# Weight sums of a Strassen stage by accumulating transfers, and product sums kept in PSUM

## The chip, the cores and the metric

The kernel runs on one core of a Trainium2 chip. The metric is the device time of one execution, in microseconds (us). Three executions of the kernel before gave a median of 2241.27 us, between 2237.95 and 2241.97.

## The reference

One step of a two-layer decoder on 576 tokens (512 of a prompt, 64 of samples) of width 1024. What matters here, per layer:

```
P = RMSNorm(x) @ w_in                      # the last columns: 4 gate blocks of 1024
up_b = o_b @ w_branch[b]                   # b = 0..3, o_b 256 wide
x += (sum_b sigmoid(G_b) * up_b) @ w_out
g, u = split(RMSNorm(x) @ w_ffn_in)        # 2816 columns each
x += (silu(g) * u) @ w_ffn_out
```

All is float32. The kernel forms each product from float16 halves: a value is a high half and a low half, and a product is three matmuls (high by high, high by low, low by high) that accumulate in PSUM.

## The kernel before, in words

Activations lie transposed: 128 features in the partitions, the 576 tokens in two halves of 288 columns (`h0`, `h1`). `self.h[k]` holds the normed input's halves for feature block k.

Two stages of each layer use one level of Strassen's scheme (Winograd's form): the last gates (`last_gates`, 8 pairs of gate columns: four of block `rt`, q = 2, then four of block `rw`, q = 3) and most of the first FFN product (`ffn`, 19 pairs: a block of g and the block of u that belongs to it). A pair has weights a11, a12, a21, a22 (each 128 x 512 numbers, 256 KB, loaded by SP) and four results of 128 x 288. Seven products, each of 12 matmuls with 288 columns, take the place of eight. Their names in the code are those of their weights: A11, A12, A22, S1, S2, S3, S4.

- `strassen_weights` (line 1684) makes the seven weights. Each is split: ScalarE (ACT) scales it into the high half (line 1692), VectorE (DVE) takes the difference as the low half (1693). Between the splits stand four sums of weights, each in place: one by an accumulating DMA that GpSimd (POOL) issues (1698), three by `tensor_tensor` on POOL (1696). A sum may only start when the split of the tile that it overwrites has been made. It is a generator; its steps are called between the products.
- `strassen` (1708) issues the seven products. ACT copies the first out of PSUM (`sp1`, 1739); seven DVE additions (`plus`, 1734) make the four results, each reading one product in PSUM.
- In the FFN, `gated` (1757) takes Silu of a g result on ACT, multiplies by u on DVE and splits the product. In the gates, a tanh is taken in place and, when a pair's four results are done, four small products with `w_branch` (`ub`, 6 matmuls each) follow; DVE multiplies, POOL adds into `mg`.
- `strassen_tokens` and `tokens_gen` make the four sums of token blocks that are the other side of the products, by differences.

Buffers: PSUM has 8 banks, four in ring `b`, two each in `g` and `r`. The FFN's weight halves have the ring `u` (23 buffers, 8 of them `self.h`). The raw weights of an odd FFN pair fill both buffers of ring `rd` (a11 with a12, a21 with a22); those of an even pair lie in three of the four `raw` buffers and one of `w`.

Loops run over pairs. While pair i's products run, the next pair's weights are made and the raw weights of the one after are loaded. The framework lays down one order of instructions for each engine when the program is built, ahead of the run, by when it takes them to be ready and by their place in the source; each engine then works through its list in that order. During the first gate pairs of a layer, the chain of the RWKV recurrence is interleaved.

Of the kernel before, what the change touches and what calls it, by code (L numbers as in the profile page):

```python
# [174 lines left out]
class Net:  # L175
# [1287 lines left out]
    def tokens_gen(self):  # L1463
# [5 lines left out]
        for k in range(4):  # L1469
            y = []  # L1470
            for o in (0, 4):
                for h in (slice(0, HW), slice(HW, T)):
                    y.append(self.t("gt", [128, HW], "mty"))
                    nc.gpsimd.tensor_tensor(y[-1], self.h[k + o][:, 0, h], self.h[k + o][:, 1, h], op=ADD)
            b11, b12, b21, b22 = y
            for i, (dst, a, b) in enumerate(((b11, b12, b11), (b12, b22, b12), (b22, b22, b11), (b21, b21, b22))):
                nc.vector.tensor_tensor(dst, a, b, op=SUB)
                t = T4[2 * (0, 2, 1, 3)[i] + k // 2][:, k % 2]
                self.split(t[:, 0], t[:, 1], dst)
            yield  # L1480

    def last_gates(self, l):
# [15 lines left out]
        def branch(bi, m):  # L1498

            out = []  # L1500
            for k in range(2):
                raw = self.t("gt", [128, 256], "braw")
                nc.sync.dma_start(out=raw, in_=t["w_branch"][l, bi][128 * k:128 * k + 128, 128 * m:128 * m + 256])
                hl = self.t("gt", [128, 2, 256], "bhl", F16)
                nc.scalar.activation(hl[:, 0], raw, AF.Copy, scale=WS)
                nc.vector.scalar_tensor_tensor(hl[:, 1], raw, WS, hl[:, 0], op0=MUL, op1=SUB)
                out.append((hl[:, 0], hl[:, 1]))
            return out
        self.sw = {}
        prep = [self.strassen_weights(i, lambda bi=p[1], m=p[3]: load(bi, m), "gs", A12="u") for i, p in enumerate(pairs)]  # L1510
        next(prep[0])
        wb = branch(pairs[0][1], 0)
        yield
        for _ in range(4):
            next(prep[0])
        yield
        for i, (q, bi, name, m) in enumerate(pairs):
            if i + 1 < len(pairs):
                next(prep[i + 1])

            def steps():
                for s in range(7):
                    if s < 4:
                        next(prep[i])
                    if s > 2 and i + 1 < len(pairs):
                        next(prep[i + 1])
                    yield
            c = yield from self.strassen(self.sw[i], lambda j, k: [self.T4[2 * j + k // 2][:, k % 2, p] for p in range(2)],
                                         steps(), "b" if q == 2 else "r", "e", lambda a: nc.scalar.activation(a, a, AF.Tanh, scale=0.5 * PH))
            nwb = branch(pairs[i + 1][1], pairs[i + 1][3]) if i + 1 < len(pairs) else None  # L1530
            for j, half in ((0, 0), (1, 1), (1, 0), (0, 1)):
                hs = slice(half * HW, half * HW + HW)
                th, mg = c[2 * j + half], self.mg[m + j]
                if q == 3 and half == j:
                    self.mh[m + j] = self.t("rs" if m < 6 else "u", [128, 2, T], f"mh{m + j}", F16)
                ps = self.psum("b", [128, HW], "ub")
                run(self.gemm(ps, lambda k: wb[k], range(2), 128 * j, 128, self.hl_rhs(self.bo[name], half)))
                u = self.t("e", [128, HW], "gu")
                nc.vector.scalar_tensor_tensor(u, th, 1.0, ps, op0=ADD, op1=MUL)  # L1539
                nc.gpsimd.tensor_tensor(mg[:, hs], mg[:, hs], u, op=ADD)  # L1540
                if q == 3:
                    mh = self.mh[m + j]
                    self.split(mh[:, 0, hs], mh[:, 1, hs], mg[:, hs], 0.5 * PA * AS)
                yield
            wb = nwb
# [119 lines left out]

    def strassen_tokens(self):
# [5 lines left out]
        for k in range(4):  # L1672
            b11, b12, b21, b22 = (self.x[k + o][:, h] for o in (0, 4) for h in (h0, h1))
            for i, (dst, a, b) in enumerate(((b11, b12, b11), (b12, b22, b12), (b22, b22, b11), (b21, b21, b22))):
                nc.gpsimd.tensor_tensor(dst, a, b, op=SUB)
                src.append(((0, 2, 1, 3)[i], k, dst))
        yield out
        for i in (3, 1, 0, 2):
            for j, k, dst in src:
                if i == j:  # L1680
                    self.split(out[i][:, k, 0], out[i][:, k, 1], dst)
            yield out

    def strassen_weights(self, key, load, ring, **rings):
# [22 lines left out]

    def strassen(self, w, t, prep, ps3, ring, then=None):
# [5 lines left out]
        def product(ring, a, rhs):  # L1714
            ps = self.psum(ring, [128, HW], "fs" + a)
            for k in range(4):
                hi, lo = rhs(k)
                nc.tensor.matmul(ps, w[a][:, 0, k], hi, start=k == 0, stop=False)  # L1718
                nc.tensor.matmul(ps, w[a][:, 0, k], lo, start=False, stop=False)  # L1719
# [223 lines left out]
```

## Time and profile before

| | |
|---|---|
| three runs, median (lowest to highest) | 2241.27 us (2237.95 to 2241.97) |
| the profiled execution: time, span | 2235.82 us, 2234.1 us |
| its mean granted TensorE clock | 0.975 |
| busy: PE, DVE, ACT, POOL | 92%, 75%, 48%, 29% of the span |

Times in the trace count from the span's start. PE is the matmul engine; its records overlap, since matmuls are pipelined, so its pace is read from successive starts. "[0.42 <-DVE sc L1734]" behind an instruction is the idle time before it and what ended it. The gate stage of the first layer lies from 536.1 to 682.0 us, its FFN pairs from 781.5 to 987.1; in the second layer they lie from 1629.4 to 1776.5 and from 1878.2 to 2086.5.

### The profile page before, as it was taken

Reading aid. Unit: us, or ns where it says so; the run is one execution under the profiler, and the core shown is the slowest. Engines: PE = TensorE matmul, PEld = TensorE weight load, DVE = VectorE, ACT = ScalarE, POOL = GpSimd, SP = SyncE. Lnnn points to the kernel's source line nnn. Section 1 sums busy time; section 2 is a strip of 40 time slices with the busy share of each in tenths; the row PEclk is TensorE's granted clock in tenths of the full one; section 3 lists DMA queues with packets and bytes.
Section 4 is the critical chain, followed back from the end, with each engine's and each line's share of the span. In section 5 each row is a group of like instructions: output and inputs, shape, how many; then the busy total and the mean of one; then the engine's idle time right before and its main releaser. Section 6 shows DMA issues by size and latency. Waiting matters only on the chain.

```text
span 2234.1 us, 42266 instructions
## 1 busy us (share of the span) xinstructions
PE 2047.3 (92%) x15754; PEld 1616.7 (72%) x15754; DVE 1677.4 (75%) x3719; ACT 1070.6 (48%) x2400; POOL 652.0 (29%) x850
## 2 busy tenths in 40 slices
PE   7988899898989999999998889889998988999998
PEld 5766676686767677777776667768776766777776
DVE  7889856868786899973488996686687768998531
ACT  6554545436454655442466344363554455554332
POOL 2212212245550544320011131222365415443000
PEclk9999999999999999999999999999999999999999
DMA  6312213333436244343421222142344443443431
GB/s 179 82 36 66 54 52 91 94 77 84 108 100 200 59 118 126 88 132 108 120 69 51 54 56 60 51 116 72 79 98 104 124 144 93 118 116 93 126 105 50
DMA packets 373497, 209.58 MB, mean 94 GB/s; under 512 B 59810, under 2 KB 360410, under 8 KB 373292
## 3 DMA queue, kind: packets, MB, share of 16 engines
q1 hardware_dynamic: 365516, 192.73, 31.1%
q0 software_dynamic: 7776, 14.16, 3.5%
q8 instruction: 124, 2.03, 0.4%
q14 instruction: 81, 0.66, 0.1%
HBM read 173.72 MB, written 16.59 MB: 85 GB/s over the span
## 4 chain that ended last, share of the span: by engine, by line
PE 47%; DVE 31%; ACT 8%; issue 7%; DMA 4%; POOL 3%; SPq 0%; DVEq 0%; ACTq 0%; POOLq 0%
PE pb L243 4%; PE pb L241 4%; PE pb L242 4%; PE xb L243 4%; PE xb L242 4%; PE xb L241 4%; DVE hA L1693 3%; DVE hS L1693 2%; DVE whl L229 2%; DVE sc L1734 2%; DVE fy L1765 2%; DVE qg L1111 2%; PE fsS L1720 2%; PE fsS L1718 2%; PE fsS L1719 2%
## 5 line engine op out<-in xcount | busy, mean ns | idle before, releaser
L241 PE MATMUL pb<-h,whl 128*128 128x288 f16 (+1 forms) x1504 | 439.9, 293 | 3.7 <-ACT h L463 2.2
L243 PE MATMUL pb<-h,whl 128*128 128x288 f16 (+1 forms) x1504 | 439.7, 293 | 2.7 <-DVE whl L229 2.7
L242 PE MATMUL pb<-h,whl 128*128 128x288 f16 (+1 forms) x1504 | 439.5, 292 | 0.6 <-DVE h L464 0.4
L229 DVE SCALAR_TENSOR_TENSOR whl<-raw,whl 128x512 f16<-128x512 f32 (+1 forms) x352 | 251.7, 725 | 132.0 <-ACT whl L228 130.3
L243 PEld LDWEIGHTS <-whl 128*128 128x128 f16 (+1 forms) x2784 | 277.3, 100 | 88.4 <-issue 11.0
L242 PEld LDWEIGHTS <-whl 128*128 128x128 f16 (+1 forms) x2784 | 276.7, 99 | 87.4 <-issue 11.0
L241 PEld LDWEIGHTS <-whl 128*128 128x128 f16 (+1 forms) x2784 | 279.0, 100 | 77.0 <-issue 3.6
L228 ACT ACTIVATE whl<-raw 128x512 f16<-128x512 f32 (+1 forms) x352 | 213.0, 616 | 167.4 <-PE pb L243 58.1
L243 PE MATMUL xb<-fa,whl 128*128 128x288 f16 x704 | 201.3, 286 | 0.0
L242 PE MATMUL xb<-fa,whl 128*128 128x288 f16 x704 | 201.3, 286 | 0.0
L241 PE MATMUL xb<-fa,whl 128*128 128x288 f16 x704 | 201.3, 286 | 0.0
L1718 PE MATMUL fsA<-h,hA 128*128 128x288 f16 x432 | 123.5, 286 | 14.4 <-DVE gu L1539 9.1
L1718 PE MATMUL fsS<-st,hS 128*128 128x288 f16 x456 | 131.1, 287 | 6.0 <-ACT hS L1692 6.0
L1720 PE MATMUL fsS<-st,hS 128*128 128x288 f16 x456 | 131.2, 288 | 0.9 <-DVE hS L1693 0.9
L1719 PE MATMUL fsS<-st,hS 128*128 128x288 f16 x456 | 131.1, 287 | 0.0
L1720 PE MATMUL fsA<-h,hA 128*128 128x288 f16 x432 | 123.6, 286 | 1.6 <-DVE hA L1693 1.6
L1719 PE MATMUL fsA<-h,hA 128*128 128x288 f16 x432 | 123.5, 286 | 0.0
L1696 POOL TENSOR_TENSOR raw<-raw 128x512 f32<-128x512 f32 x52 | 79.5, 1529 | 133.8 <-DVE hA L1693 129.7
L1718 PEld LDWEIGHTS <-hS 128*128 128x128 f16 x864 | 85.1, 99 | 35.5 <-ACT hS L1692 14.1
L1693 DVE SCALAR_TENSOR_TENSOR hA<-sraw,hA 128x512 f16<-128x512 f32 x110 | 101.5, 930 | 10.4 <-ACT hA L1692 9.7
L1696 POOL TENSOR_TENSOR sraw<-sraw 128x512 f32<-128x512 f32 x60 | 89.9, 1501 | 50.0 <-DVE hA L1693 45.5
L1720 PEld LDWEIGHTS <-hS 128*128 128x128 f16 x864 | 85.2, 99 | 24.6 <-DVE hS L1693 3.0
(487 smaller groups left out, 5271.1 us busy)
## 6 DMA issues: line engine op xcount, KB each, us to landing
raw<-in_w_in SPq DMA_DIRECT2D x208, 256.0 KB
sraw<-in_w_ffn_in SPq DMA_DIRECT2D x40, 512.0 KB
raw<-in_w_ffn_out SPq DMA_DIRECT2D x80, 256.0 KB
raw<-in_w_ffn_in SPq DMA_DIRECT2D x78, 256.0 KB
x<-xd SPq DMA_DIRECT2D x32, 288.0 KB
raw<-sraw POOLq DMA_DIRECT2D x34, 256.0 KB, 3.3
sraw<-in_w_in SPq DMA_DIRECT2D x32, 256.0 KB
raw<-in_w_out SPq DMA_DIRECT2D x32, 256.0 KB
```

What stands on the lines that cost most here:

```text
L228: nc.scalar.activation(hl[:, 0, :n], raw[:, :n], AF.Copy, scale=WS)
L229: nc.vector.scalar_tensor_tensor(hl[:, 1, :n], raw[:, :n], WS, hl[:, 0, :n], op0=MUL, op1=SUB)
L241: nc.tensor.matmul(ps, wh, hi, start=i == 0, stop=False)
L242: nc.tensor.matmul(ps, wh, lo, start=False, stop=False)
L243: nc.tensor.matmul(ps, wl, hi, start=False, stop=i == len(ks) - 1)
L1111: nc.vector.tensor_tensor(qo, qq, ee, op=MUL)
L1693: nc.vector.scalar_tensor_tensor(hl[:, 1], a, WS, hl[:, 0], op0=MUL, op1=SUB)
L1696: nc.gpsimd.tensor_tensor(dst, a, b, op=op)
L1718: nc.tensor.matmul(ps, w[a][:, 0, k], hi, start=k == 0, stop=False)
L1719: nc.tensor.matmul(ps, w[a][:, 0, k], lo, start=False, stop=False)
L1720: nc.tensor.matmul(ps, w[a][:, 1, k], hi, start=False, stop=k == 3)
L1734: nc.vector.tensor_tensor(o, a, p, op=ADD)
```

## The change

The scheme is written with other signs, so that all four sums of weights are plain additions: a11 += a21, a21 += a22, a22 += a11 (already summed), a12 += a22 (already summed). All four are accumulating DMAs issued by POOL; no POOL arithmetic on weights is left. One of four token sums becomes an addition, another changes its operands' order, and one of four token blocks is split with a factor of -1.

The products A11, S2, S3 and, in the next pair, A22 accumulate in one PSUM bank (X); S1 and, in the next pair, S4 in another (Z); A12 has its own (Y). ACT copies X after A11 (p1), after S2 (u2) and after S3 (u3); DVE adds three times: p1 + Y, u3 + Z, u2 + Z after S4; the fourth result is read in X itself. The order is A11, A22 of the pair before, S1, S4 of the pair before, S2, A12, S3. Results are used one by one (`then`), between products. PE does the same 84 matmuls per pair. In the gates the weight A22 moves from ring `gs` to `u`.

```diff
 def strassen_weights(self, key, load, ring, **rings):
-        def add(dst, a, b, op):
-            nc.gpsimd.tensor_tensor(dst, a, b, op=op)
-        yield
-        nc.gpsimd.dma_start(out=a21, in_=a22, accum_op=ADD)
-        yield
-        for name, a, op0, op1 in (("A11", a11, a21, a11), ("A22", a22, a22, a11), ("A12", a12, a12, a11)):
-            split(name, a)
-            add(a, op0, op1, SUB)
-            yield
-        for name, a in (("S2", a11), ("S1", a21), ("S3", a22), ("S4", a12)):
-            split(name, a)
-            yield
+        def add(dst, a):
+            nc.gpsimd.dma_start(out=dst, in_=a, accum_op=ADD)
+        yield
+        split("A11", a11)
+        add(a11, a21)
+        yield
+        add(a21, a22)
+        split("A22", a22)
+        yield
+        add(a22, a11)
+        split("A12", a12)
+        yield
+        split("S1", a21)
+        yield
+        add(a12, a22)
+        split("S2", a22)
+        yield
+        split("S3", a11)
+        yield
+        yield
+        split("S4", a12)
+        yield
+    def strassen_prep(self, gens, key, q):
+        if q < 4:
+            step(key)
+        if q > 2:
+            step(key + 1)
+        if q == 3:
+            step(key + 2)
 def strassen(...):
-        p1 = self.t("gt", [128, HW], "sp1")
-        nc.scalar.copy(p1, (yield from product("b", "A11", b(0, h0))))
-        c11 = plus(p1, (yield from product("b", "A12", b(4, h0))), "sc11")
-        p4 = yield from product("g", "A22", tt(3))
-        u2 = plus(p1, (yield from product("b", "S2", tt(1))), "su2")
-        p5 = yield from product("g", "S1", tt(0))
-        u4 = plus(u2, p5, "su4")
-        u3 = plus(u2, (yield from product(ps3, "S3", tt(2))), "su3")
-        c22 = plus(u3, p5, "sc22")
-        c21 = plus(u3, p4, "sc21")
-        c12 = plus(u4, (yield from product(ps3, "S4", b(4, h1))), "sc12")
+        for key in [*keys, None]:
+            new = key is not None
+            if new:
+                prep(key, 0)
+                x = self.psum(rx, [128, HW], "fsX")
+                yield from product(key, "A11", x, b(0, h0), True)
+                p1 = kept(rc, x, "sp1")
+                prep(key, 1)
+            if old:
+                okey, ox, oz, ou2 = old
+                yield from product(okey, "A22", ox, lambda k: tt(okey, 3, k), False)
+                yield from then(okey, 2, ox)
+            if new:
+                prep(key, 2)
+                z = self.psum(rz, [128, HW], "fsZ")
+                yield from product(key, "S1", z, lambda k: tt(key, 0, k), True)
+                prep(key, 3)
+            if old:
+                yield from product(okey, "S4", oz, b(4, h1), False)
+                yield from then(okey, 1, plus(ou2, oz))
+            if new:
+                prep(key, 4)
+                yield from product(key, "S2", x, lambda k: tt(key, 1, k), False)
+                u2 = kept(rc, x, "su2")
+                prep(key, 5)
+                y = self.psum(ry, [128, HW], "fsY")
+                yield from product(key, "A12", y, b(4, h0), True)
+                yield from then(key, 0, plus(p1, y))
+                prep(key, 6)
+                yield from product(key, "S3", x, lambda k: tt(key, 2, k), False)
+                u3 = kept(rc, x, "su3")
+                yield from then(key, 3, plus(u3, z))
+                old = key, x, z, u2
 def ffn(self, l):
+        def then(m, quarter, c):
+            parts[m, quarter] = c
+            if quarter < 2:
+                nc.scalar.activation(c, c, AF.Silu, scale=PH)
+            if quarter in (1, 2):
+                half = 2 - quarter
+                times(m, half, parts.pop((m, half)), parts.pop((m, 2 + half)), -PH)
+            return ()
...
```

`kept` is an ACT copy from PSUM, `plus` a DVE addition in place, `times` the DVE multiply in place with the split of its result.

## Rows read from the trace of the kernel before

**Rows 1.** The page, part 1: each engine's busy time.
```profile
PE 2047.3 (92%) x15754; PEld 1616.7 (72%) x15754; DVE 1677.4 (75%) x3719; ACT 1070.6 (48%) x2400; POOL 652.0 (29%) x850
```

**Rows 2.** Windows: length; busy PE, PEld, DVE, ACT, POOL (instructions); clock; DMA share; GB/s.
```profile
536.10:682.00 145.90, 129.24 (x1010) 101.67 (x1008) 120.68 (x227) 73.51 (x171) 82.34 (x81) 0.99 0.42 109
781.50:987.10 205.60, 196.76 (x1591) 155.25 (x1591) 195.12 (x332) 102.78 (x219) 87.00 (x67) 1.00 0.42 108
1629.40:1776.50 147.10, 132.34 (x1000) 102.77 (x998) 118.58 (x226) 73.84 (x171) 81.37 (x78) 0.95 0.41 108
1878.20:2086.50 208.30, 199.39 (x1602) 157.04 (x1602) 197.25 (x336) 102.77 (x219) 87.08 (x67) 0.99 0.42 109
```

**Rows 3.** Timeline of PE in FFN pairs: start, length (us), instruction, idle before.
```profile
903.70 0.28 PE L1718 MATMUL fsA<-st,hA 128*128 128x288 f16 x1 [0.86 <-DVE sc L1734]
914.61 0.28 PE L1718 MATMUL fsA<-st,hA 128*128 128x288 f16 x1 [0.46 <-DVE sc L1734]
...
985.44 0.29 PE L1720 MATMUL fsS<-st,hS 128*128 128x288 f16 x1
...
987.65 0.29 PE L1720 MATMUL fsS<-h,hS 128*128 128x288 f16 x1
```

**Rows 4.** Tile fsA, whole span: PE idle before it (us, times), by releaser.
```profile
  DVE sc L1734: 10.8, 16
  DVE gu L1539: 9.1, 6
```

**Rows 5.** Tile fsS, whole span: PE idle before it, by releaser.
```profile
  ACT hS L1692: 12.7, 4
```

**Rows 6.** Timeline of DVE in an FFN pair.
```profile
915.81 0.45 DVE L1765 SCALAR_TENSOR_TENSOR fy<-sc,fsg 128x288 f32<-128x288 f32 x1
...
917.15 1.93 DVE L1765 SCALAR_TENSOR_TENSOR fy<-sc,fsg 128x288 f32<-128x288 f32 x1
```

**Rows 7.** Timeline of POOL beside it.
```profile
917.18 1.57 POOL L1696 TENSOR_TENSOR sraw<-sraw 128x512 f32<-128x512 f32 x1
```

**Rows 8.** Sources L1734, L1692, L1693 and tile fsA: ns lowest/median/highest.
```profile
L1734 DVE TENSOR_TENSOR sc<-su,fsS x108: 440/453/455, 556.2 to 2086.4; 128x288 f32<-128x288 f32 x108
L1739 ACT COPY sp<-fsA x54: 374/381/402, 541.1 to 2079.3; 128x288 f32<-128x288 f32 x54
L1692 ACT ACTIVATE hS<-sraw x130: 612/615/641, 541.9 to 2080.5; 128x512 f16<-128x512 f32 x130
L1693 DVE SCALAR_TENSOR_TENSOR hS<-sraw,hS x130: 677/683/1759, 546.9 to 2081.6; 128x512 f16<-128x512 f32 x130
```

**Rows 9.** Source L1698, the accumulating DMA: its issues on POOL, its landing.
```profile
L1698 POOL DMA_DIRECT2D raw<-sraw x34: 862/881/1035, 533.6 to 2047.0; - x34
DMA to landing us min/median/max: 3.2/3.3/5.4
```

**Rows 10.** The page, part 3: packets, MB, share of 16 engines' span.
```profile
q1 hardware_dynamic: 365516, 192.73, 31.1%
q0 software_dynamic: 7776, 14.16, 3.5%
```

**Rows 11.** Timelines of SP, POOL and DVE around the FFN's first pair.
```profile
780.00 0.92 SPq L1787 DMA_DIRECT2D raw<-in_w_ffn_in  x2
...
784.35 0.88 POOL L1698 DMA_DIRECT2D raw<-sraw  x1 [0.67 <-DMA raw<-in_w_ffn_in]
...
781.65 0.68 DVE L1693 SCALAR_TENSOR_TENSOR hA<-sraw,hA 128x512 f16<-128x512 f32 x1
```

**Rows 12.** Timelines of ACT and PE near the first FFN stretch's end.
```profile
967.37 0.63 ACT L228 ACTIVATE whl<-raw 128x512 f16<-128x512 f32 x1 [6.36 <-DMA raw<-in_w_ffn_out]
...
970.51 0.30 PE L1718 MATMUL fsS<-st,hS 128*128 128x288 f16 x1 [2.82 <-ACT hS L1692]
```

**Rows 13.** Timeline of POOL in a late FFN pair.
```profile
949.68 0.86 POOL L1698 DMA_DIRECT2D raw<-sraw  x1 [6.05 <-DVE hA L1693]
950.24 4.53 POOL L1696 TENSOR_TENSOR sraw<-sraw 128x512 f32<-128x512 f32 x3
```

More of the change, by code (lines that the diff above doesn't have):

```diff
@@ L1509, in last_gates @@
+            yield
         self.sw = {}
-        prep = [self.strassen_weights(i, lambda bi=p[1], m=p[3]: load(bi, m), "gs", A12="u") for i, p in enumerate(pairs)]
-        next(prep[0])
-        wb = branch(pairs[0][1], 0)
+        gens = {i: self.strassen_weights(i, lambda bi=p[1], m=p[3]: load(bi, m), "gs", A12="u", A22="u") for i, p in enumerate(pairs)}
+        next(gens[0])
         yield
         for _ in range(4):
-            next(prep[0])
+            next(gens[0])
+        next(gens[1])
@@ L1516, in last_gates @@
         yield
[L1517 to L1526, printed above, removed]
-                    yield
[L1528 to L1543, printed above, removed]
-                yield
-            wb = nwb
@@ new lines, in last_gates, with prep, then @@
+        branches = {}
+        def prep(i, q):
+            self.strassen_prep(gens, i, q)
+            if q == 0:
+                branches[i] = branch(i)
+            if q in (0, 3):
+                next(branches[i])
+        def then(i, quarter, c):
+            q, bi, name, m = pairs[i]
+            j, half = quarter // 2, quarter % 2
+            hs = slice(half * HW, half * HW + HW)
+            th = self.t("e", [128, HW], "gth") if quarter == 2 else c
+            nc.scalar.activation(th, c, AF.Tanh, scale=(-0.5 if j else 0.5) * PH)
+            mg = self.mg[m + j]
+            if q == 3 and half == j:
+                self.mh[m + j] = self.t("rs" if m < 6 else "u", [128, 2, T], f"mh{m + j}", F16)
+            ps = self.psum("b", [128, HW], "ub")
+            run(self.gemm(ps, lambda k: wb[i][k], range(2), 128 * j, 128, self.hl_rhs(self.bo[name], half)))
+            u = self.t("e", [128, HW], "gu")
+            nc.vector.scalar_tensor_tensor(u, th, 1.0, ps, op0=ADD, op1=MUL)
+            nc.gpsimd.tensor_tensor(mg[:, hs], mg[:, hs], u, op=ADD)
+            if q == 3:
+                mh = self.mh[m + j]
+                self.split(mh[:, 0, hs], mh[:, 1, hs], mg[:, hs], 0.5 * PA * AS)
+            yield
@@ L1547, in add_x @@
+        yield from self.strassen(range(len(pairs)), lambda i, j, k: [self.T4[2 * j + k // 2][:, k % 2, p] for p in range(2)], prep,
+                                 lambda i: ("g", "b" if pairs[i][0] == 2 else "r", "b", "e"), then)
     def add_x(self, m, half, ps, store, last=False):
@@ L1680, in strassen_tokens @@
                 if i == j:
-                    self.split(out[i][:, k, 0], out[i][:, k, 1], dst)
+                    self.split(out[i][:, k, 0], out[i][:, k, 1], dst, -1.0 if i == 1 else 1.0)
             yield out
@@ L1711, in strassen, with step, product @@
+        yield
+    def strassen_prep(self, gens, key, q):
+        def step(k):
+            if k in gens:
+                next(gens[k], None)
+        if q < 4:
+            step(key)
+        if q > 2:
+            step(key + 1)
+        if q == 3:
+            step(key + 2)
+    def strassen(self, keys, tt, prep, rings, then):
         nc = self.nc
         h0, h1 = slice(0, HW), slice(HW, T)
[L1714 to L1715 removed]
+        def product(key, a, ps, rhs, start):
+            w = self.sw[key][a]
@@ L1791, in ffn @@
         self.sw = {}
-        prep = [self.strassen_weights(m, lambda m=m: load(m), "u") for m in range(3, nm)]
-        next(prep[0])
+        prep = {m: self.strassen_weights(m, lambda m=m: load(m), "u") for m in range(3, nm)}
+        next(prep[3])
         for half in range(2):
```

90 lines of the change are left out of this document (38 added, 52 removed).

## The prediction

> **What bounds the kernel now.** I read the page's busy times first. PE is busy 92% of the span, DVE 75%, ACT 48%, POOL 29% [rows 1]; PE's records overlap, so this says which engine to look at, not how much is left. The change touches only the Strassen stages, so next come windows over the two gate and the two FFN stretches, 706.9 us together [rows 2]. In the FFN stretches DVE is busy 195.12 of 205.6 us and 197.25 of 208.3, ACT about 103 and POOL 87: DVE is as full as PE there. Third, PE's pace: between the starts 985.44 and 987.65 lie 18 matmuls, so one takes 0.123 us, a product of 12 takes 1.47 us and a pair of 84 takes 10.3 us [rows 3]. Two pairs begin 10.9 us apart (903.70 and 914.61), each after an idle that a DVE addition ended [rows 3]. 19 pairs at PE's pace are 195.7 us; the stretches lose 9.9 and 12.6 us, 22.5 together. Fourth, who ended PE's idle times before Strassen products, over the whole span: the DVE additions 10.8 us, the gates' DVE multiply 9.1, ACT's splits 12.7 [rows 4, 5]. So PE sets the end, DVE holds it up by about 1 us in the middle pairs, and there is little to win: 22.5 us in the FFN and at most the 31.5 us that PE is not busy in the gate stretches (145.9 - 129.24 and 147.1 - 132.34).
>
> DVE is so full partly because of POOL. A multiply of 0.45 us took 1.93 us when it began at 917.15 with a POOL addition from 917.18 to 918.75 [rows 6, 7], and a split's median of 683 ns has a maximum of 1759 [rows 8].
>
> **The change part by part.**
>
> *DVE, ACT, PE.* Per pair DVE makes 3 additions in place of 7: 4 x 0.45 = 1.8 us less [rows 8], and the collisions with POOL's weight sums go. ACT makes two more copies, 2 x 0.38 = 0.8 us [rows 8], over the 102.78 / 19 = 5.4 us it is busy per pair now: 6.2 of 10.3. Both then have room, and the wait of PE for DVE's additions goes. PE's 84 matmuls stay. Each of u2 and u3 must be copied before the next product enters X, but one product (A12, or the next A11), 1.47 us, lies between, and the copy takes 0.38: hidden as long as ACT is free when S2 and S3 end. After the last pair A22 follows S3 at once: about 0.5 us, four times, left out of the sum. The signs of the token sums change no count; a split with a factor of -1 takes the same kind of DVE instruction as the weights' splits. These cost nothing I can see.
>
> *POOL.* Three additions per pair leave, three DMA issues of 0.88 us [rows 9] come. POOL is not on the path by its busy time. But each of these issues waits for what came before, and POOL works through its list in order: in the gates its additions into `mg` stand behind them.
>
> *The chain of sums.* This is what decides. a21 += a22 overwrites what a11 += a21 reads; a22 += a11 needs its result; a12 += a22 needs the third. So the four transfers of a pair run one after the other, each landing 3.3 us after its issue (median; 5.4 at most) [rows 9]; now it is one such transfer and POOL additions. How long will one take when there are four per pair? The queue of these DMAs took 3.5% of the span for 54 transfers, 0.035 x 2234 / 54 = 1.45 us of all 16 engines each; the loads took 31.1% for 192.73 MB, 3.6 us per MB [rows 10]. A pair then asks 4 x 1.45 + 3.6 = 9.4 of 10.3 us. A transfer that meets another during most of its 1.45 us is stretched by up to that: I take 0.6 us more, 3.9 us, between 3.3 and 5.4, nearest the median since most of its time is no transfer.
>
> The Trainium skill, "DMA: Bandwidth & Descriptors" (Two DMAs through the same engine are not ordered), says that a dependent DMA must be issued only after the earlier one's semaphore, whatever queue they share; that speaks against any overlap within the chain. The same page's fit (Anatomy of one DMA) of 2.0 us plus bytes over 436 GB/s would give 2.6 us per link, an estimate of 10.4 us per chain; the 3.3 us of the row is longer, and the row decides.
>
> Now the loop through the raw buffers. An odd FFN pair fills both `rd` buffers, so the next odd pair's load waits for this pair's S4 split. A load: four issues from 780.00 on, and the sum that needed the last of the tiles it reads went at 784.35, after a wait for that landing [rows 11], so 4.4 us; I take 4.5. Then the A11 split, 0.62 + 0.68 = 1.3 us [rows 8], four transfers 15.6, the S4 split 1.3: 22.7 us for two pairs, 11.35 per pair against PE's 10.3. With 3.3 per transfer it is 20.3, just inside 20.6; with 5.4 it is 28.7, 14.4 per pair.
>
> A lead at the start pays part of it. The third pair's A11 split is made at 781.65 [rows 11]; three transfers later, at 794.0, and a split after that, at 795.3, its S2 is ready; PE wants it at 781.5 + 2 x 10.3 + 4 x 1.47 = 808.0. The lead is 12.7 us, 17 pairs use 17 x 1.05 = 17.9, so 5.2 us per FFN stretch come late.
>
> *ACT's order.* The splits of S1, S2 and S4 now wait for a DMA, in ACT's fixed list, with the copies of u2 and u3 behind them, and PE waits for those. The trace has a case: ACT stood 6.36 us at a split whose load had not landed, and PE 2.82 us at 970.51 for the Strassen split behind it [rows 12], 0.44 of ACT's wait. If each of the four links is 0.6 us longer than the order allows for (my assumption: the order cannot know what the engines' queues add), ACT waits 2.4 us per pair and PE 0.44 x 2.4 = 1.05 us, 20 us per stretch. Bounds: 0 if the order allows for it, 46 us if PE waits as long as ACT.
>
> *FFN.* 195.7 + 5.2 + 20.0 = 220.9 us, against 205.6 and 208.3: 15.3 + 12.6 = 27.9 us more. Bounds: -22.5 (chain and ACT hidden), and with 5.4 per link (lead 12.7 - 4.5 = 8.2) 17 x 4.1 - 8.2 = 61.5 over 195.7, so +101 for both.
>
> *Gates.* The small products go between the others, so the wait for the gates' DVE multiply, 9.1 us, goes [rows 4]; I take 2 us more off the waits of the interleaved RWKV chain, as DVE is freer. A pair takes 145.9 / 8 = 18.2 us here, and the chain with its two splits also 18.2, with two pairs' raw buffers: I cost its lateness at nothing (bound: 1.05 x 16 = 17 us). The clock granted is 0.95 in the second gate stretch [rows 2]; a fuller PE could get back up to 7 us of that, counted in the 31.5. So -11, between -31 and +6.
>
> Sum: +27.9 - 11 = +17 us on the profiled execution's 2235.8, 2253; the median shown lies 5.4 us higher, so 2258 us (+0.75%).
>
> **The rivals.**
>
> *A, the chain is hidden.* If a transfer stays at 3.3 us (loop 20.3 < 20.6) and the order allows for it, PE runs at its pace: -22.5 - 11 = -33.5, 2208 us. For it: half the profile's DMA time is free (share 0.42), the lead is 12.7 us, and DVE and ACT have room. Against it: 9.4 of 10.3 us of DMA time, and a margin of 0.3 us per two pairs.
>
> *B, they cancel.* With half of ACT's effect, 10 us per stretch, the FFN takes 210.9, +7.9, and the gates give 11: -3 us, 2238.
>
> *C, POOL's list runs the chains one after another.* If the four sums of a pair all stand ahead of the next pair's first, no pair can go faster than 4 x 3.9 = 15.6 us: 17 x 5.3 - 12.7 = 77 us per stretch over 195.7, +132 - 11, 2362 us. It decides from 2.6 us per link on. For it: POOL stood idle 6.05 us before one such issue, with three sums of another pair behind it [rows 13]. Against it: POOL has little else to do now, and its list before alternates between pairs.
>
> *D, DVE starves the issue.* If DVE's work held up the descriptors, each link would be as the longest now, 5.4 us: +101 - 11, 2331 us. The issues took 881 ns in the median beside a DVE that was 95% busy, 1035 at most [rows 2, 9], which speaks against it. It is the rule of the Trainium skill, "SBUF — State Buffer" (SBUF: two separate sides, the trap "DVE blocks DMA"): POOL writes descriptors through a port that some DVE instructions lock; the trace does not show it. The same page (Who interferes with whom) says that two DVE inputs from SBUF and a POOL read exclude each other; the 1.93 us of [rows 6] agree.
>
> That the edit fails to take the POOL additions or the four DVE additions away is excluded by the diff.
>
> **How the numbers follow.** Forecast 0.42, A 0.36, B 0.10, C 0.08, D 0.04. A measurement tells about 0.2%, 4.5 us, from no change. Slower: 0.42 + 0.08 + 0.04 = 0.54; same 0.10; faster 0.36. The range, 2200 to 2310 us, leaves out C and D, 0.12, and some 0.06 beyond A's and the forecast's own price. The forecast's own range is 2246 to 2300.
>
> **What would show it.** Right: the two FFN stretches grow by some 15 us; PE's idle before Strassen products is ended by ACT (splits and the copies of X), ACT's by accumulating DMAs, with landings near 3.9 us; DVE's busy time there falls below 150 us; POOL's additions on weights are gone; the gates get shorter. Wrong: pairs 10.3 us apart to the end of the stretch (A), landings at 3.3 us, or PE idle that DVE still ends. Landings of 5 us would be D, sums of a pair all ahead of the next one's first on POOL would be C.

## The result, and the profile after

The changed kernel takes 2546.49 us (median of four runs, 2542.81 to 2554.34) against 2241.44 us for the kernel before on the same chip: ratio 1.1366, 95% interval 1.1339 to 1.1392. Slower was forecast, but 2258 us; the loss is 305 us, not 17. The profile is that of the longest of the four executions.

The page of the kernel after, parts 1 and 3, beside [rows 1, 10]: PE does the same 15754 matmuls and is busy longer, DVE and POOL are less busy, and the queue of the accumulating DMAs has grown from 3.5% to 13.1% of a longer span.

```profile
PE 2150.4 (84%) x15754; PEld 1652.9 (65%) x15754; DVE 1502.6 (59%) x3503; ACT 1112.5 (44%) x2508; POOL 553.3 (22%) x850
...
q1 hardware_dynamic: 365516, 192.73, 27.3%
q0 software_dynamic: 31104, 56.64, 13.1%
```

The windows of the kernel after over the gate and FFN stretches, columns as in [rows 2]. The FFN stretches are 130 us longer each and the gates 24 to 25, 309.6 of the span's 318.5 us. DVE is busy 138 us in place of 195, the granted clock is 0.88 and 0.86 in place of 1.00 and 0.99.

```profile
536.40:706.00 169.60, 136.21 (x959) 102.21 (x957) 97.20 (x187) 77.29 (x183) 63.74 (x78) 0.91 0.59 135
811.10:1147.00 335.90, 236.72 (x1608) 167.47 (x1606) 137.75 (x263) 122.22 (x263) 61.07 (x71) 0.88 0.52 111
1789.80:1962.00 172.20, 139.62 (x976) 105.01 (x975) 97.77 (x190) 78.01 (x184) 63.17 (x77) 0.91 0.58 131
2067.20:2406.00 338.80, 240.82 (x1611) 170.75 (x1609) 138.11 (x264) 122.01 (x263) 61.07 (x71) 0.86 0.52 110
```

POOL's timeline over two FFN pairs of the kernel after, where [rows 13] showed sums of two pairs mixed. Each issue waits for the landing of the one before; the first of the next pair (880.39, and again 900.76) comes behind all four of this one and waits for a split.

```profile
867.42 0.86 POOL L1703 DMA_DIRECT2D sraw<-sraw  x1 [2.97 <-DMA sraw<-sraw]
871.17 0.86 POOL L1703 DMA_DIRECT2D sraw<-sraw  x1 [2.89 <-DMA sraw<-sraw]
874.90 0.86 POOL L1703 DMA_DIRECT2D sraw<-sraw  x1 [2.87 <-DMA sraw<-sraw]
880.39 0.86 POOL L1703 DMA_DIRECT2D raw<-raw  x1 [4.63 <-DVE hA L1700]
886.25 0.86 POOL L1703 DMA_DIRECT2D raw<-sraw  x1 [5.00 <-DMA raw<-raw]
890.05 0.86 POOL L1703 DMA_DIRECT2D sraw<-raw  x1 [2.94 <-DMA raw<-sraw]
894.46 0.86 POOL L1703 DMA_DIRECT2D raw<-sraw  x1 [3.55 <-DMA sraw<-raw]
900.76 0.86 POOL L1703 DMA_DIRECT2D sraw<-sraw  x1 [5.45 <-DVE hA L1700]
```

ACT's timeline of the same pair says which split. At 878.14 S4 is split, after a wait for the fourth sum; the next pair's A11 split stands directly behind it, at 878.68, and the copy of u2 (880.57) only behind that.

```profile
874.39 1.15 ACT L1699 ACTIVATE hS<-sraw 128x512 f16<-128x512 f32 x2 [2.81 <-DMA sraw<-sraw]
...
878.14 0.63 ACT L1699 ACTIVATE hS<-sraw 128x512 f16<-128x512 f32 x1 [2.27 <-DMA sraw<-sraw]
878.68 0.61 ACT L1699 ACTIVATE hA<-raw 128x512 f16<-128x512 f32 x1
...
880.57 0.38 ACT L1761 COPY su<-fsX 128x288 f32<-128x288 f32 x1
```

So there is a loop: A11 split, four sums one after another, S4 split behind the last, the next A11 split behind that. From the rows: 3.75 and 3.73 us between the issues of an odd pair, 3.24 from the last to the S4 split and 2.25 to the next pair's first issue; an even pair goes from 880.39 to 900.76, 20.4 us, since its first link took 5.9. The mean over a stretch is 17.5 us per pair where PE needs 10.3 [rows 3].

Why that first link is longer can be read from SP's timeline and from windows over four links (columns as in [rows 2]): the landing of the fourth sum and the S4 split let go two loads of 512 KB each, which SP issues from 878.31 on (one merged line), and they still move when the next pair's first sum does (third window: 192 GB/s, where the other links have 80 or 81).

```profile
878.31 1.58 SPq L1831 DMA_DIRECT2D sraw<-in_w_ffn_in  x2
```

```profile
867.42:870.70 3.28, 3.28 (x29) 2.62 (x27) 0.39 (x1) 0.04 (x1) 0.86 (x1) 1.00 0.44 80
871.17:874.40 3.23, 3.23 (x29) 2.57 (x27) 1.06 (x2) 0.42 (x3) 0.86 (x1) 1.00 0.45 81
880.39:886.20 5.81, 5.21 (x22) 3.19 (x22) 2.63 (x6) 1.74 (x5) 0.86 (x1) 0.50 0.75 192
886.25:889.50 3.25, 3.25 (x25) 2.48 (x24) 0.00 (x0) 0.40 (x1) 0.85 (x1) 0.89 0.45 81
```

Counted from the packets of both FFN stretches, 68 of 142 sums met no load, and their last packet ended 2.9 us after the issue in the median; 16 met more than 0.3 MB of loads, all of them first links of even pairs, and took 4.0 to 7.3 us. Sums of the same tiles in the gates that met 0.3 MB or less took 3.0 to 3.6.

PE of the same pair: it stood 5.47 us for the copy of u2, and its twelve matmuls then took 3.04 us, not 1.63, at a granted clock of 0.50 (the third window above).

```profile
873.89 1.63 PE L1751 MATMUL fsY<-h,hA 128*128 128x288 f16 x12
881.00 3.04 PE L1751 MATMUL fsX<-st,hS 128*128 128x288 f16 x12 [5.47 <-ACT su L1761]
```

What PE waited for before Strassen products over the whole span of the kernel after (us, times, longest; the two largest), in place of [rows 4, 5]: DVE's additions are gone from the top, ACT stands there.

```profile
PE fsX L1751 <- ACT su L1761: 118.0, 44, 6.3
PE fsZ L1751 <- ACT hS L1699: 55.1, 18, 6.5
```

And the source of the accumulating DMAs in the kernel after, who waited for them and the landings, beside [rows 9]:

```profile
  ACT hS L1699: 400.4, 149
  POOL sraw L1703: 259.2, 89
  POOL raw L1703: 167.4, 44
...
DMA to landing us min/median/max: 3.2/3.3/7.8
```

### The profile page after: what moved, and what is told of

Read it like the earlier page. It is cut to its first block, busy times and chain, and to the rows that moved or that the text cites. A ratio compares the mean times of both kernels' runs of the same rounds, so it can differ in the third digit from the quotient of the medians.

```text
span 2552.6 us, 42357 instructions
## 1 busy us (share of the span) xinstructions
PE 2150.4 (84%) x15754; PEld 1652.9 (65%) x15754; DVE 1502.6 (59%) x3503; ACT 1112.5 (44%) x2508; POOL 553.3 (22%) x850
## 3 DMA queue, kind: packets, MB, share of 16 engines
q0 software_dynamic: 31104, 56.64, 13.1%
## 5 line engine op out<-in xcount | busy, mean ns | idle before, releaser
L1751 PEld LDWEIGHTS <-hS 128*128 128x128 f16 x2592 | 271.2, 106 | 281.3 <-issue 119.2
L1751 PEld LDWEIGHTS <-hA 128*128 128x128 f16 x1944 | 204.6, 106 | 135.7 <-issue 35.0
L1751 PE MATMUL fsX<-st,hS 128*128 128x288 f16 x912 | 150.3, 320 | 97.8 <-ACT su L1761 64.8
L1700 DVE SCALAR_TENSOR_TENSOR hS<-sraw,hS 128x512 f16<-128x512 f32 x130 | 98.3, 768 | 207.8 <-ACT hS L1699 207.6
L1700 DVE SCALAR_TENSOR_TENSOR hS<-raw,hS 128x512 f16<-128x512 f32 x86 | 68.5, 797 | 180.0 <-ACT hS L1699 179.5
L1699 ACT ACTIVATE hS<-sraw 128x512 f16<-128x512 f32 x130 | 79.8, 627 | 213.9 <-DMA sraw<-sraw 144.3
L1703 POOL DMA_DIRECT2D sraw<-sraw x96 | 82.7, 862 | 324.3 <-DMA sraw<-sraw 168.0
L1751 PE MATMUL fsX<-h,hA 128*128 128x288 f16 x648 | 107.4, 315 | 27.0 <-ACT hA L1699 23.2
L1751 PE MATMUL fsZ<-st,hS 128*128 128x288 f16 x456 | 83.5, 341 | 48.9 <-ACT hS L1699 48.6
L1751 PE MATMUL fsY<-h,hA 128*128 128x288 f16 x648 | 104.8, 305 | 0.0
```

Of the source, the lines that this page charges most:

```text
L1699: nc.scalar.activation(hl[:, 0], a, AF.Copy, scale=WS)
L1700: nc.vector.scalar_tensor_tensor(hl[:, 1], a, WS, hl[:, 0], op0=MUL, op1=SUB)
L1703: nc.gpsimd.dma_start(out=dst, in_=a, accum_op=ADD)
L1751: nc.tensor.matmul(ps, w[:, part, k], x, start=start and k == i == 0, stop=k == 3 and i == 2, skip_group_check=not start)
```

## The experiments

Fourteen more kernels ran. Times are medians, ratios against the kernel before on the same chip. "FFN" is the first FFN stretch, from the start of its first Strassen matmul to the end of its last, and "gates" the same for the first gate stretch.

| run | us | ratio (95%) | FFN | gates |
|---|---|---|---|---|
| before | 2241 | | 206.4 | 141.3 |
| after | 2546.49 | 1.1366 (1.1339 to 1.1392) | 336.1 | 173.8 |
| psum_pool | 2307.69 | 1.0303 (1.0272 to 1.0334) | 227.1 | 157.3 |
| dma_old_products | 2542.84 | 1.1354 (1.1315 to 1.1392) | 331.0 | 167.6 |
| no_chain | 2307.86 | 1.0293 (1.0261 to 1.0325) | 234.0 | 149.9 |
| early_start | 2467.76 | 1.1010 (1.0977 to 1.1043) | 294.9 | 174.0 |
| interleaved | 2384.41 | 1.0642 (1.0619 to 1.0666) | 256.7 | 175.6 |
| late_silu | 2308.42 | 1.0306 (1.0279 to 1.0332) | 227.9 | 160.4 |
| dve_copies | 2320.45 | 1.0361 (1.0335 to 1.0387) | 230.8 | 160.9 |
| two_links | 2416.10 | 1.0783 (1.0751 to 1.0815) | 280.5 | 167.1 |
| pinned | 2276.90 | 1.0171 (1.0152 to 1.0190) | 216.5 | 157.0 |
| hybrid | 2256.38 | 1.0083 (1.0066 to 1.0101) | 216.6 | 144.2 |
| interleaved_pinned | 2370.29 | 1.0595 (1.0572 to 1.0618) | 260.2 | 170.4 |
| hybrid2 | 2236.73 | 0.9981 (0.9966 to 0.9995) | 206.1 | 144.6 |
| last_by_dma | 2272.54 | 1.0142 (1.0124 to 1.0160) | 222.9 | 144.4 |
| next_first | 2252.84 | 1.0053 (1.0035 to 1.0071) | 212.7 | 141.1 |

**Which part of the change.** Two theories were the serial chain of transfers (T1) and the product scheme with its copies on ACT (T3); the transfers' own load (T2) was the other.

*psum_pool*: the products of after, the four sums on POOL.

```diff
-            nc.gpsimd.dma_start(out=dst, in_=a, accum_op=ADD)
+            nc.gpsimd.tensor_tensor(dst, dst, a, op=ADD)
```

> The changed kernel with its four sums of weights as POOL additions; the products in PSUM as changed. Theory 1 (a pair's four transfers, its last split and the next pair's first split stand in one line, 17.5 us per FFN pair): a POOL chain is 4 x 1.5 + 2.6 = 8.6 us, under PE's 10.3, so the FFN stretches fall from 336 to about 205 us and the whole to 2215 to 2240 us. Theory 2 (the accumulating DMAs load the DMA engines and the loads come late): the same. Theory 3 (the new order of products and ACT's copies of X hold PE up, as its 118 us of waits for the copies say): the FFN pairs stay above 13 us, the whole above 2340 us.

2307.69 us, between what T1 and T2 gave and what T3 gave: the DMAs make 239 us of the loss, and 66 us stay without any.

*dma_old_products*: the products, copies and additions of before (DVE), the four sums by DMA. The edit is shown against after, for one of the seven products.

```diff
-                yield from product(key, "S2", x, lambda k: tt(key, 1, k), False)
-                u2 = kept(rc, x, "su2")
+        u2 = plus(p1, (yield from product("b", "S2", tt(1))), "su2")
```

> The kernel before with its seven separate products and DVE additions, only its sums of weights as the four accumulating DMAs (with the new signs). Theories 1 and 2: FFN pairs of 16 to 18 us as in the changed kernel, the whole 2480 to 2560 us. Theory 3: about 2241 us, at most 2270.

2542.84 us, the same as after and in the range of T1 and T2. The two parts don't add: while the chain is the bound, the waits for the copies hide beneath it.

*no_chain*: as after, but each DMA adds a constant tile, so that none waits for another's result; the sums of weights are left out.

```diff
-            nc.gpsimd.dma_start(out=dst, in_=a, accum_op=ADD)
+            nc.gpsimd.dma_start(out=dst, in_=self.cst[:, :512].rearrange("p (k c) -> p k c", k=4), accum_op=ADD)
```

> The changed kernel, each accumulating DMA reading a constant tile instead of a weight tile (the sums of weights are not formed): as many DMAs, as many bytes, but none waits for another. Theory 1: a pair's sums take one landing of 3.3 us, the FFN pairs fall to PE's 10.3 us, the whole to 2200 to 2235 us. Theory 2: the DMA load is the same, the FFN pairs stay above 14 us and the whole above 2400 us.

2307.86 us with the same number of issues and bytes written, and landings of 4.2 us in the median, longer than in after. The time lies between the two ranges expected: T1's left out the 66 us. Taking the dependence away takes away the 239 us, with the transfers' load as it was: it is the order, one behind the other, that costs them.

**Where the chain closes.** *early_start*: in the FFN the next pair's A11 split and sums are written ahead of this pair's S4 split.

```diff
+        def early(m, q):
+            for k, at in ((m, (0, 1)), (m + 1, (0, 1, 2, 4, 5, 6)), (m + 2, (2,))):
+                if q in at and k in prep:
+                    next(prep[k], None)
```

> The changed kernel with the FFN's preparation moved in the source: the next pair's A11 split and first sums come ahead of this pair's S4 split, so that two chains of transfers can overlap. Theory 1 with the source's order as the cause: FFN pairs of 11.4 (the raw buffers' loop of 22.7 us for two pairs) to 13 us, the whole 2310 to 2380 us. If the order is not free but set by full buffers: pairs stay at 17 us, about 2540 us. Theory 2: overlapped chains gain nothing, about 2540 us.

2467.76 us, 78 of the 305 us, and outside every range expected. The next pair's first sum no longer waited for this pair's S4 split, but POOL's list still had four and four. Pairs now lie 15.5 us apart in the mean, about four links. This is its timeline, an odd pair from its first issue to the next pair's, 14.9 us:

```profile
884.56 0.86 POOL L1703 DMA_DIRECT2D sraw<-sraw  x1 [1.62 <-DVE hA L1700]
888.83 0.86 POOL L1703 DMA_DIRECT2D sraw<-sraw  x1 [3.42 <-DMA sraw<-sraw]
892.59 0.86 POOL L1703 DMA_DIRECT2D sraw<-sraw  x1 [2.90 <-DMA sraw<-sraw]
896.34 0.86 POOL L1703 DMA_DIRECT2D sraw<-sraw  x1 [2.88 <-DMA sraw<-sraw]
899.49 0.88 POOL L1703 DMA_DIRECT2D raw<-raw  x1 [2.29 <-DVE sp L1814]
```

*interleaved*: the chains of two pairs made to alternate in POOL's list, by holding the FFN's DMAs and splits to the order of the source.

```diff
+            for o, n, at in ((0, 9, 0), (2, 1, 0), (1, 4, 1), (1, 5, 2), (2, 2, 4), (1, 6, 4), (1, 7, 5), (2, 3, 6)):
+                if q == at:
+                    upto(m + o, n)      # pair m + o up to its step n
+            pin(nc.gpsimd.dma_start(out=dst, in_=a, accum_op=ADD))   # keep_in_program_order
```

> The changed kernel, but in the FFN the chains of two pairs are made to alternate in POOL's list: next pair's sum 1, this pair's sum 4, next pair's sum 2 and 3, with the splits of ACT pinned in the same order. Gates as in the changed kernel. Theory (the prediction's step that failed is that two pairs' chains overlap; POOL's list has all four sums of a pair ahead of the next pair's first): only three links of 3.75 us then stand one after another per pair, 11.3 us, so an FFN pair falls from 17.5 to 11.3 to 12.5 us, each FFN stretch from 336 to some 215 to 245 us, and the time from 2546 to 2310 to 2365 us. Rival (the transfers hinder each other when two are under way, or the loads come late): landings above 4.5 us, pairs of 14 us or more, 2420 us or more.

2384.41 us, 162 us less than after: the mechanism is as expected, its size missed by 20 us. POOL's timeline shows why: an issue now follows another pair's within a microsecond, but the links of one pair, 896.05 to 900.22 to 904.71, took 4.2 and 4.5 us (the second ended with a DVE instruction, not a landing), and the next pair's first sum waited to 910.27 for its split. Landings were 3.8 us in the median over the span, 3.3 in after, so transfers that overlapped took longer, if less than the rival had it.

```profile
896.05 0.86 POOL L1703 DMA_DIRECT2D sraw<-sraw  x1 [3.99 <-DMA sraw<-raw]
896.59 1.21 POOL L1703 DMA_DIRECT2D raw<-sraw  x1
900.22 0.86 POOL L1703 DMA_DIRECT2D sraw<-sraw  x1 [2.42 <-DMA sraw<-sraw]
904.71 0.86 POOL L1703 DMA_DIRECT2D sraw<-sraw  x1 [3.63 <-DVE sp L1824]
910.27 0.86 POOL L1703 DMA_DIRECT2D raw<-raw  x1 [4.70 <-DVE hA L1700]
```

*two_links*: sums 1 and 2 by DMA, 3 and 4 on POOL.

```diff
-            nc.gpsimd.dma_start(out=dst, in_=a, accum_op=ADD)
+            if dst is a11 or dst is a21:
+                nc.gpsimd.dma_start(out=dst, in_=a, accum_op=ADD)
+            else:
+                nc.gpsimd.tensor_tensor(dst, dst, a, op=ADD)
```

> The changed kernel with sums 1 and 2 as accumulating DMAs and sums 3 and 4 as POOL additions. Theory (an FFN pair is the serial chain where that is longer than the rest): 2 x 3.75 + 2 x 1.6 + 2.6 for the two splits that close the loop = 13.3 us per pair against 17.5 with four links and 11.4 with none, so each FFN stretch 255 to 265 and the time 2370 to 2395 us with the gates' share. Rival (each accumulating DMA costs its share wherever it stands): halfway between 2308 and 2546, 2415 to 2440 us. If only the number of transfers behind one another beyond three decides: under 2330 us.

2416.10 us, in the rival's range. The loop gives 13.3 us only with 3.75 us for every link; POOL's timeline has 5.84 us (882.28 to 888.12) for the first link of an even pair, which makes 16.0 us from there to the next pair's first, at 898.29; and ACT's A11 split in between waited 1.52 us for PE, which the theory's loop does not have. So the theory's price was too low (pairs lay 14.3 to 14.6 us apart in the mean), and this run can't tell a chain from a price per DMA. Two later runs bear on that.

**The 66 us without a DMA.** In psum_pool an FFN pair takes 11.4 us. ACT's and PE's timelines there (one fence each): the copy of u3 stood behind a Silu that waited for DVE, and PE waited 0.96 us for the copy.

```profile
871.92 0.44 ACT L1866 ACTIVATE sp<-sp 128x288 f32<-128x288 f32 x1 [0.92 <-DVE sp L1765]
872.27 0.38 ACT L1761 COPY su<-fsX 128x288 f32<-128x288 f32 x1
```

```profile
872.71 1.63 PE L1751 MATMUL fsX<-st,hA 128*128 128x288 f16 x12 [0.96 <-ACT su L1761]
```

*late_silu*: that Silu written behind the copy of u3.

```diff
-                yield from then(key, 0, plus(p1, y))
                 prep(key, 6)
                 ...
                 u3 = kept(rc, x, "su3")
+                yield from then(key, 0, plus(p1, y))
```

> The four sums as POOL additions (2308 us), and the use of the first result (Silu in the FFN, tanh and small product in the gates) written behind the copy of u3 instead of ahead of S3. Theory (the 66 us that the product scheme costs without any DMA sum are copies of X behind waiting instructions in ACT's list): PE's wait of 0.97 us per FFN pair for the copy of u3 goes, pairs at 10.4 to 10.6 us, each FFN stretch from 227 to 207 to 213, the time 2270 to 2285 us. Rival (the copies are late because DVE's additions are late, beside POOL's additions): the wait moves to another product, 2295 us or more.

No change, nor could there be: the framework, which orders by when it takes things to be ready, left the Silu ahead of the copy (873.44 and 873.79 in this run's ACT timeline). So the run tells nothing between theory and rival.

*dve_copies*: the copies of u2 and u3 on DVE.

```diff
-            nc.scalar.copy(o, ps)
+            nc.vector.tensor_copy(o, ps) if name[1] == "u" else nc.scalar.copy(o, ps)
```

> The four sums as POOL additions (2308 us), and the copies of u2 and u3 made by DVE instead of ACT. Theory (ACT's list holds them up): DVE takes them behind at most one or two splits of 0.7 us, PE's wait for the copies of X falls from 79 us to under 40, time 2260 to 2290. Rival (DVE is late too, since POOL's additions slow it): PE waits as long for DVE, 2300 to 2330 us.

2320.45 us: PE waits 78.7 us for DVE's copies in place of 78.8 for ACT's. The rival was right: DVE's timeline has the copy of u2 at 872.63 behind a split of 1.39 us and a multiply of 1.52 us, both beside POOL's four additions (867.63 to 873.84), where [rows 8, 6] have 0.68 and 0.45 for them.

*pinned*: late_silu, with ACT's copies, Silus and splits of the FFN held to the order of the source.

```diff
-            nc.scalar.copy(o, ps)
+            self.pin(ring == "gt", nc.scalar.copy(o, ps))   # keep_in_program_order
```

> The four sums as POOL additions, and in the FFN ACT's copies of X, Silus and weight splits held to the order of the source, in which each copy of X comes ahead of the next split and the Silu of the first result behind the copy of u3. (Writing the Silu later in the source alone left ACT's list as it was: 2308 us, the same wait of 0.95 us per pair.) Theory (PE waits because the copies of u2 and u3 stand in ACT's list behind instructions that themselves wait): no wait of PE for a copy of X in the middle pairs, FFN pairs of 10.3 to 10.5 us, also the late ones that took 13.6 to 15.6, each FFN stretch 203 to 212 us instead of 227, time 2255 to 2280 us. Rival (DVE's multiply beside POOL's additions sets the pace, 11.4 us, whatever ACT's order): FFN 222 us or more, 2295 us or more.

2276.90 us, in the range, though not by the steps named, and the FFN stretch, 216.5 us, above its own range: the late pairs of 13.6 to 15.6 us fell to 11.2, but for one, the middle ones only from 11.4 to 11.25, since now the copy of u2 stood behind a Silu and a split of the product that waited 1.20 and 0.86 us for DVE.

*hybrid* has the FFN of pinned (`grown` is its `strassen`, `sum_weights` its `strassen_weights`) and the gates of before:

```diff
+        prep = {m: self.sum_weights(m, lambda m=m: load(m), "u") for m in range(3, nm)}
+        run(self.grown(range(3, nm), lambda m, i, k: (T4[i][:, k, 0], T4[i][:, k, 1]),
```

*interleaved_pinned* is interleaved with the copies and Silus held in order as well:

```diff
-            nc.scalar.copy(o, ps)
+            i = nc.scalar.copy(o, ps)
+            if ring == "gt":
+                self.tc.keep_in_program_order(i)
```

> The FFN as in the run with ACT's order held (POOL additions, product sums in PSUM), the gates as in the kernel before. Theory (the product scheme costs the gates 14 us each and can gain in the FFN once the copies are in time): gates 146 us each, FFN 203 to 212, time 2225 to 2250 us, about that of before. If the FFN keeps its 227 us: 2280 us.

> The alternating chains of accumulating DMAs (2384 us), and in the FFN ACT's copies of X and Silus held to the order of the source as well. Theory (three links of 3.75 to 4.3 us a pair, 11.3 to 12.9 us, remain the bound; what PE waits for copies beyond that goes): FFN pairs of 11.3 to 12.9 us, stretches 215 to 245 us, time 2300 to 2362 us. Rival (the alternating chains are at their bound already, 13.4 us a pair): within 10 us of 2384.

hybrid: 2256.38 us, 6 above its range: the gates come back from 157.0 to 144.2 us, so the changed gates cost 12 to 13 us each (146.1 for 158.4 in the second layer); the FFN kept its 216.6. In pinned, whose gates were not held in order, PE waited 14.2 and 14.4 us there for copies of X, which is of that size; no run moved those copies.

interleaved_pinned: 2370.29 us, 14 less than interleaved, between the ranges of theory and rival. The two FFN stretches together are the same (511.5 and 512.1 us, in a profile of this run's longest execution): holding the copies in order won nothing there, which speaks for the rival's bound without showing what sets it.

*hybrid2*: hybrid with the second result's Silu and split behind the copy of u2.

```diff
-                yield from then(okey, 1, plus(ou2, oz))
             if new:
                 prep(key, 4)
                 yield from product(key, "S2", x, lambda k: tt(key, 1, k), False)
                 u2 = kept(rc, x, "su2")
+            if old:
+                yield from then(okey, 1, plus(ou2, oz))
```

> As the run with the gates of before and ACT's order held in the FFN (2256 us), with the Silu and the split of the second result moved behind the copy of u2 too. There PE still waited 0.8 us per pair for the copy of u2, which stood behind a Silu and a split of the product, both waiting for DVE. Theory (each wait of PE for a copy of X is a place in ACT's list): the 0.8 us go, FFN pairs of 10.3 to 10.6 us, stretches 199 to 207 us, time 2222 to 2240 us, at or below the kernel before. Rival (DVE is the bound behind it): pairs stay at 11 us or more, 2250 us or more.

2236.73 us: the wait for the copy of u2 goes; one of 0.3 us for that of u3 is left, with the middle pairs 10.75 us apart. PE's wait for copies of X falls to 13.3 us; psum_pool had 78.8, of them 51.8 in the FFN (26.0 and 25.8) and the rest in the gates, which have no such copies in hybrid2.

```profile
PE fsX L1751 <- ACT su L1761: 78.8, 47, 5.9
```

```profile
PE fsX L1815 <- ACT su L1825: 13.3, 28, 2.3
```

The time is that of before or 0.2% under it, so the 66 us are all won back: in the FFN by places in ACT's list, in the gates by going back to their old form, which does not say what in the new one cost them. The FFN stretches of hybrid2 in windows (columns as before): DVE is busy 173 us where before it was 195 [rows 2], and the stretches are only 0.3 and 1.6 us shorter.

```profile
784.20:990.30 206.10, 198.82 (x1604) 156.24 (x1602) 173.24 (x262) 119.57 (x262) 103.56 (x69) 1.00 0.33 97
1882.40:2088.60 206.20, 200.20 (x1604) 156.98 (x1602) 173.05 (x262) 119.58 (x262) 103.61 (x69) 0.99 0.33 97
```

**One DMA, and one exchange.** *last_by_dma*: hybrid2 with the fourth sum by DMA.

```diff
-            nc.gpsimd.tensor_tensor(dst, dst, a, op=ADD)
+            if dst is a12 and key > 3:
+                nc.gpsimd.dma_start(out=dst, in_=a, accum_op=ADD)
+            else:
+                nc.gpsimd.tensor_tensor(dst, dst, a, op=ADD)
```

> The same with the fourth sum of a pair (a12 += a22), whose result is wanted last, as an accumulating DMA and the other three as POOL additions. Theory (such a DMA costs only what waits for its landing): its 3.75 us stand in place of 1.6 us at the end of a chain that has some 3 us left, so within 10 us of the run without it. Rival (each accumulating DMA costs its share, 240 us for four, 60 us each, half of that outside the gates): 20 us or more slower than the run without it.

2272.54 us, 36 us more than hybrid2, the rival's side. But the loop had no 3 us to spare: ACT's timeline has the S4 split waiting for the DMA and the next A11 split at once behind it, and POOL's three additions then took 4.53 us (868.34 to the end), so that the next loop began 11.0 us on (one fence each).

```profile
866.29 0.63 ACT L1759 ACTIVATE hS<-raw 128x512 f16<-128x512 f32 x1 [2.39 <-DMA raw<-sraw]
866.83 1.13 ACT L1759 ACTIVATE hA<-sraw 128x512 f16<-128x512 f32 x2
```

```profile
868.34 4.53 POOL L1766 TENSOR_TENSOR sraw<-sraw 128x512 f32<-128x512 f32 x3 [6.03 <-DVE hA L1760]
...
879.38 1.64 POOL L1766 TENSOR_TENSOR raw<-raw 128x512 f32<-128x512 f32 x1 [4.54 <-DVE hA L1760]
```

*next_first*: the same with only the two splits exchanged.

```diff
-        if q < 4:
-            step(key)
         if q > 2:
             step(key + 1)
+        if q < 4:
+            step(key)
```

> The run with the fourth sum as an accumulating DMA (2273 us), with one exchange in ACT's list: the next pair's A11 split stands ahead of this pair's S4 split, not behind it. Theory (the loop is A11 split, sums one after another, S4 split behind the last sum, and the next A11 split behind that; 11.5 us with one DMA, 8.9 without, 17.5 with four): the exchange opens the loop, the DMA's landing is then waited for by the S4 split alone, PE's wait for copies falls to some 20 us from 45, FFN pairs 10.5 to 11.0 us, stretches 204 to 212, time 2234 to 2255 us. Rival (the DMA itself costs it, in landing or contention, wherever the next A11 stands): 2265 us or more.

2252.84 us, in the theory's range: 20 of the 36 us go, with the DMA as it was; FFN 212.7 and 214.7 us. ACT's timeline: A11 is split ahead, and S4 still waits, in some pairs, for the landing (4.5 us in the median of these DMAs), with the A22 split and the copy of u2 behind it. PE's wait for the copies is 28.2 us, between 45.3 in last_by_dma and 13.3 in hybrid2: the 16 us left are mostly that wait.

```profile
876.54 0.61 ACT L1759 ACTIVATE hA<-sraw 128x512 f16<-128x512 f32 x1
878.88 0.63 ACT L1759 ACTIVATE hS<-raw 128x512 f16<-128x512 f32 x1 [1.72 <-DMA raw<-sraw]
879.41 0.61 ACT L1759 ACTIVATE hA<-sraw 128x512 f16<-128x512 f32 x1
879.93 0.38 ACT L1828 COPY su<-fsX 128x288 f32<-128x288 f32 x1
```

## Why the prediction was wrong

*What failed: "the loop through the raw buffers".* It was worked out as 22.7 us for two pairs, 11.35 per pair, which takes the chains of two pairs to run beside each other; less the lead, it was to cost 5.2 us per FFN stretch. In the lists the chains ran one after another: pairs lay 17.5 us apart, and the first FFN stretch took 336.1 us, 140 above PE's 195.7, where the sum had 5.2 for this loop and 20.0 for ACT's order. The lead did not show: the first pair already took 23.0 us (its first product starts at 811.1, the next pair's at 834.1).

The reason why a pair's four transfers can't overlap held: POOL's timeline above has each issue behind the landing of the one before, after 2.9 us of idling. The rule that was weighed there, of the Trainium skill, "DMA: Bandwidth & Descriptors" (Two DMAs through the same engine are not ordered), asks for just that, and the trace agrees. What was not asked is what stands ahead of the next chain's first split. no_chain, interleaved and next_first show it from three sides: take the dependence away (239 of the 305 us go), make the chains alternate (162), open the loop of one DMA (20 of its 36).

*The link* of 3.9 us came out near by luck. It was to be a landing of 3.3 us that other transfers stretch by 0.6. Landings stayed at 3.3 us in the median, which the prediction had named as a sign of being wrong; the 3.75 us are such a landing and the way to the next issue. Loads did stretch a link, but one in eight, by 2 us.

*Rival C* had this mechanism with a chance of 0.08, and too small a price, 2362 us. It put the serial order in POOL's list alone, 15.6 us a pair; early_start, which opens the way through ACT, measured 15.5. In the kernel after, the loop closes through ACT, over an A11 and an S4 split more, and the lead that C took off did not show. What was given against it, that POOL's list had alternated before, counted for nothing: that list was made for other instructions.

*"Hidden as long as ACT is free"* failed as well. ACT was busy 122 of the first FFN stretch's 336 us, and yet PE waited 46.8 us there for copies of u2 and u3 (118.0 over the span): the copy's place in the list decides, not the busy share. That term was set at nothing; where the chain is not the bound (psum_pool), PE waits 78.8 us for these copies and the kernel is 66 us slower than before.

*Gates*, forecast at -11 together, became +49 by the windows. Their chains were costed at nothing, at 18.2 of 18.2 us; no_chain takes the gates from 173.8 and 173.9 us to 149.9 and 156.0. And the product scheme, forecast as a gain, stands in gates that take 12 to 13 us longer each where no sum is a DMA (pinned against hybrid).

*ACT's order*, 1.05 us a pair, can't be told apart as a term: ACT's splits waited 400.4 us for the transfers, within the loop.

*What held:* slower, though not for the reason given; DVE's busy time under 150 us and PE's idle before Strassen products no longer ended by its additions; that idle ended by ACT, ACT's by accumulating DMAs. "What would show it" named the sign of C, and the trace has it. Landings of 5 us were to be D's sign: the first links of even pairs have them, but beside loads, with DVE busy 2.63 of 5.81 us in the window above. D itself was hardly tried, since DVE was busy only 41% of the stretch.

*Left open:* the meeting of sums and loads is read from the packets; no run took the loads away. By the same count, 16 of the 36 single DMAs of last_by_dma met no load (2.9 us to the last packet in the median), and the other 20 did (4.3). What the lower clock adds to the time was not separated from the waits that bring it, nor what in the changed gates costs them 12 to 13 us.

## What to carry to other kernels

Where a chain of transfers is handed from one loop turn to the next, find the instruction that starts the next chain and read what stands ahead of it in its engine's list; if that waits for this chain's end, the turn costs the whole chain, even where there are buffers for two. A copy that frees the accumulator of the engine that sets the pace belongs ahead of everything in its list that can wait; an engine's low busy share does not show that it is there. Ask, too, which load an instruction lets go, and which transfer that load will meet. Freeing an engine that is full (22 to 24 us of DVE in each FFN stretch in hybrid2) bought next to nothing here.

## What the runs showed of the hardware

An accumulating DMA of 256 KB within SBUF, waited for by the next, cost 3.75 us per link from issue to issue in the kernel after, 0.86 of it the issue; a POOL addition of the same size 1.4 to 1.6 in the median (late_silu). With two or more under way the landings grew from 3.3 us in the median to 3.8 (interleaved) and 4.2 (no_chain); beside 0.8 MB of loads, one link took 5.86. After PE had stood 5.47 us, the granted clock was at 0.50, 1.2 of 2.4 GHz, from 880.39 to 886.20, and twelve matmuls took 3.04 us in place of 1.63; the FFN stretches had a mean of 0.88 and 0.86, against 1.00 and 0.99 in hybrid2's.
